# Low parts of singly used weight blocks by an accumulating DMA in place of a DVE subtraction

## The chip, the cores and the metric

One core of a Trainium2 chip runs the whole program in one launch. The metric is the device time of one execution in microseconds (us); lower is better.

## The reference

The reference runs two layers of a hybrid backbone, in float32, over 640 tokens: 512 latent tokens and 128 context tokens, which share all weights. Cut to what matters:

```python
def mixer(h, p, rope, ctx_kv):
    z = h @ p['w_in']
    u_pool, cb, cc, ch, q, k, v, gates = jnp.split(z, [...], axis=-1)
    ...
    g = jax.nn.sigmoid(gates).reshape(B, L, N_BRANCH, D_MODEL)
    merged = (g[:, :, 0] * (pool_out @ p['w_br_pool'])
              + g[:, :, 1] * (conv_out @ p['w_br_conv'])
              + g[:, :, 2] * (attn_out @ p['w_br_attn']))
    return merged @ p['w_o'], k, v

def layer(x, cvec, p, rope, ctx_kv):
    mod = jax.nn.silu(cvec) @ p['w_ada'] + p['b_ada']
    sh1, sc1, g1, sh2, sc2, g2 = [m[:, None, :] for m in jnp.split(mod, 6, axis=-1)]
    h = rmsnorm(x, p['norm1_g']) * (1 + sc1) + sh1
    out, k, v = mixer(h, p, rope, ctx_kv)
    x = x + g1 * out
    h2 = rmsnorm(x, p['norm2_g']) * (1 + sc2) + sh2
    ffn = (jax.nn.silu(h2 @ p['w_gate']) * (h2 @ p['w_up'])) @ p['w_down']
    return x + g2 * ffn, k, v
```

The width is 1024 and the FFN's hidden width 2816. The outputs are both groups' final activations and the new keys and values.

## The kernel before

**Products.** Activations stand transposed, features on the 128 partitions and the 640 tokens in the free dimension, in two halves of 320. A weight block is 128 output features of one matrix: 128 partitions with 1024 columns (8 chunks of 128), or 768 or 512 of them. TensorE multiplies in a rounded 32-bit type (F32R). To keep float32's accuracy each operand is split into a high part, its rounding, and a low part, the rest, and three products are added: high x high, low x high, high x low. So a block of 8 chunks takes 2 x 8 x 3 = 48 matmuls of 320 columns (`mm`, L682).

**The way of a weight block.** `plan` lists all blocks in the order of use. For a block that is used once (`Unit`), SP loads the raw values into one of four RAW buffers (tile `wr`); when two of six WQ buffers (tile `wq`, one for the high and one for the low part) are free, ACT casts the block to the high part (L351) and DVE subtracts that from the raw block into the low part (L352), both in `half_split`. Then the RAW buffer goes back and PE may start. After its last matmul the two WQ buffers go back. The first block of a layer and the first of its FFN (`big`) take one large buffer (`g`) instead. There are 196 such blocks. The first three of the program carry a `gate`, an event that holds their load back until the start has issued its own loads.

```python
    def half_split(hi, lo, src, n):
        yield act(n, lambda: nc.scalar.copy(hi, src), slack=WEIGHT)
        yield dve(n, lambda: nc.vector.tensor_sub(lo, src, hi), slack=WEIGHT)
```

Most gate and up blocks of the FFN come as a `Pair`: their quarters and four sums of quarters serve 7 products in place of 8 (L585), each quarter in one WQ buffer. Their splits also use `half_split`.

**The stages of a layer.** First 14 blocks of w_in for keys, values, queries, pooling and convolution, with attention between them. Then the merge: for each of 8 output blocks m three gate blocks (8 chunks), a branch block that holds the pool's and the convolution's 2 chunks each, and an attention block of 4 chunks; behind each of the three branch products DVE multiplies by the gate (L1479) and adds up (L1485), and the sum is split again (L300 on ACT, L301 on DVE). PE takes them, from the third m on, in the order gate, pool, gate, convolution, gate, attention, that is 48 + 12 + 48 + 12 + 48 + 24 = 192 matmuls. Then 8 blocks of w_o, and the FFN in four groups of gate and up blocks, each followed by 8 down blocks (6 chunks, in the last group 4).

**The modulation (ada).** The vectors mod = silu(c) @ w_ada are not made on PE, but in the background, mostly during the merges: `ada_back` loads half rows of w_ada (256 KB, tile `p`, two buffers) and DVE reduces each against the two conditioning vectors with a fused multiply and sum (L752, tile `junk`, one call for each vector).

```python
            yield d
            while quiet[0]:
                yield 500.0
            for v in range(2):
                ...
                yield ttr(out, w, s[v][q], start, 512, BACK)
            yield 700.0
            PP.put(i)
```

**What sets the order.** The kernel's code is a set of generators. When the program is built, `_Order` runs them against assumed costs (in ns) and lays down each engine's instructions in the order of its own clock. An operation names its engine and cost, `slack` moves its rank in the queue (BACK puts the reductions behind all else), and LAG is added before the next step of the same generator. A load of n bytes is booked at n / 350 ns on a queue `dma` plus 2100 of LAG. On the chip each engine keeps that order and waits on semaphores where data are not there. So a change of one assumed cost moves the order on all engines. SP's queue carries all loads in one order (L284); POOL has only a few small operations.

## Time and profile before

| what | value |
|---|---|
| time, median of 3 runs (lowest to highest) | 1877.96 us (1876.62 to 1879.35) |
| the profiled execution's own time | 1883.69 us |
| its span | 1881.7 us |
| PE, DVE, ACT, POOL busy, share of the span | 97%, 76%, 43%, 2% |
| plain DMA queue | 194.86 MB, 31.7% of the 16 engines |
| HBM read | 188.01 MB |

The span is the time from the first to the last instruction; the profiled execution's time is 2 us longer, and 5.7 us longer than the median of the runs. Busy shares are means over stages that differ, and a busy PE is not always at its peak, so the rows below are taken by stretch. All loads are issued by SP, none by POOL.

### The profile page before, as it was taken

What the parts mean: (1) busy time and instruction counts of PE and PEld (TensorE: products, weight loads), DVE (VectorE), ACT (ScalarE), POOL (GpSimd) and SP (SyncE); (2) the same over time, 40 slices, a digit from 0 to 9 for tenths busy, and PEclk for the clock granted to TensorE, in tenths of its full rate; (3) what the DMA queues carried; (4) which work ended last, traced back from release to release, by engine and by line L of the source; (5) the groups of instructions that cost most, each with busy time, mean ns of one, the idle gap of its engine ahead of it and who ended that gap; (6) DMA issues with size and microseconds to landing.
All of it is one profiled execution on the core that took longest, in us unless ns stands there. A gap on an engine that the chain in (4) does not pass through costs nothing.

```text
span 1881.7 us, 31312 instructions
## 1 busy us (share of the span) xinstructions
PE 1827.1 (97%) x12427; PEld 1794.6 (95%) x12427; DVE 1424.9 (76%) x2663; ACT 816.6 (43%) x1437; POOL 40.1 (2%) x79
## 2 busy tenths in 40 slices
PE   7999999998999999999999999999999999999997
PEld 4999999998989999999989999999999899999997
DVE  7798777887799785775778986888748858667575
ACT  5587622222364252442466775222235525335254
POOL 0100000000000000000002000000000000000000
PEclk9999999999999999999999999999999999999998
DMA  8210144555413322222242012554541222222221
GB/s 321 85 36 31 49 159 146 166 159 205 138 45 116 115 85 84 79 82 81 70 154 74 32 40 80 168 168 165 172 134 35 79 85 85 81 78 83 85 68 68
DMA packets 77107, 196.84 MB, mean 105 GB/s; under 512 B 8865, under 2 KB 12961, under 8 KB 76961
## 3 DMA queue, kind: packets, MB, share of 16 engines
q1 hardware_dynamic: 76962, 194.86, 31.7%
q8 instruction: 97, 1.59, 0.3%
q14 instruction: 48, 0.39, 0.1%
HBM read 188.01 MB, written 5.51 MB: 103 GB/s over the span
## 4 chain that ended last, share of the span: by engine, by line
PE 68%; DVE 17%; DMA 8%; issue 4%; ACT 2%; POOL 0%; SPq 0%; DVEq 0%; POOLq 0%; ACTq 0%
PE ps L682 35%; PE ps L585 25%; DMA p<-in_w_ada 7%; DVE junk L752 5%; DVE wq L352 4%; PE ps L1199 2%; PE ps L1237 2%; PE ps L1217 2%; DVE u L1485 1%; DVE t L1479 1%; PE ps L1672 1%; DVE g L555 1%; PE ps L1010 1%; DVE g L298 0%; DVE g L301 0%
## 5 line engine op out<-in xcount | busy, mean ns | idle before, releaser
L682 PE MATMUL ps<-g,wq 128*128 128x320 f32 x7488 | 1150.0, 310 | 16.9 <-DVE wq L352 6.7
L682 PEld LDWEIGHTS ps<-g,wq 128*128 128x128 f32 x7488 | 1106.9, 188 | 24.2 <-DVE wq L352 10.2
L585 PE MATMUL ps<-g,wq 128*128 128x320 f32 x3360 | 500.8, 311 | 7.3 <-DVE wq L352 4.8
L585 PEld LDWEIGHTS ps<-g,wq 128*128 128x128 f32 x3360 | 497.4, 189 | 9.7 <-DVE wq L352 5.6
L351 ACT CAST wq<-wr 128x512 fp32r<-128x512 f32 (+2 forms) x312 | 244.6, 784 | 314.3 <-PE ps L682 241.9
L352 DVE TENSOR_TENSOR wq<-wr,wq 128x512 fp32r<-128x512 f32 (+2 forms) x312 | 278.0, 891 | 46.6 <-ACT wq L351 45.5
L1524 DVE SCALAR_TENSOR_TENSOR g<-ps,mod,g 128x128 f32<-128x128 f32 (+3 forms) x172 | 83.3, 523 | 160.6 <-PE ps L682 160.6
L752 DVE CUSTOM_DVE_ANT_0 junk<-p,k,vec 128x512 f32<-128x512 f32 x160 | 120.0, 750 | 49.2 <-DMA p<-in_w_ada 46.0
L351 ACT CAST wq<-u 128x512 fp32r<-128x512 f32 x160 | 98.8, 621 | 123.9 <-PE ps L585 59.2
L752 DVE CUSTOM_DVE_ANT_0 junk<-p,k,part 128x512 f32<-128x512 f32 x160 | 120.0, 750 | 27.4 <-DMA p<-in_w_ada 23.8
L352 DVE TENSOR_TENSOR wq<-u,wq 128x512 fp32r<-128x512 f32 x160 | 109.3, 688 | 22.5 <-ACT wq L351 21.8
L1474 ACT ACTIVATE t<-ps 128x640 f32<-128x640 f32 x32 | 22.6, 705 | 176.2 <-PE ps L682 176.2
L642 ACT COPY t<-ps 128x320 f32<-128x320 f32 x80 | 34.2, 427 | 75.7 <-PE ps L585 75.7
L1207 ACT ACTIVATE p<-ps,st 128x640 f32<-128x640 f32 x64 | 51.0, 796 | 25.4 <-DVE st L1205 22.6
L298 DVE TENSOR_TENSOR g<-ps,g 128x640 fp32r<-128x640 f32 (+1 forms) x68 | 54.8, 809 | 5.9 <-ACT g L297 5.5
L916 ACT ACTIVATE g<-t,mod,gain 128x320 fp32r<-128x320 f32 (+5 forms) x108 | 55.6, 572 | 5.7 <-DVE t L897 3.3
L1205 DVE TENSOR_REDUCE st<-ps 128x1 f32<-128x640 f32 x64 | 52.2, 815 | 3.9 <-PE ps L1199 3.6
L297 ACT CAST g<-ps 128x640 fp32r<-128x640 f32 (+1 forms) x68 | 46.4, 684 | 19.9 <-PE ps L1217 16.4
L300 ACT ACTIVATE g<-u 128x640 fp32r<-128x640 f32 x16 | 11.8, 739 | 94.9 <-DVE u L1485 94.9
L301 DVE SCALAR_TENSOR_TENSOR g<-t,g 128x640 fp32r<-128x640 f32 x44 | 36.2, 823 | 17.7 <-ACT g L300 17.7
L1199 PE MATMUL ps<-k,g 128*128 128x320 f32 x256 | 48.9, 313 | 0.3 <-ACT p L1207 0.2
L647 DVE TENSOR_TENSOR t<-t,ps 128x320 f32<-128x320 f32 x80 | 38.7, 484 | 10.3 <-PE ps L585 7.8
(157 smaller groups left out, 1442.1 us busy)
## 6 DMA issues: line engine op xcount, KB each, us to landing
p<-in_w_ada SPq DMA_DIRECT2D x160, 256.0 KB, 2.9
wr<-in_w_in SPq DMA_DIRECT2D x76, 512.0 KB, 3.6
wr<-in_w_gate SPq DMA_DIRECT2D x44, 512.0 KB, 3.3
wr<-in_w_up SPq DMA_DIRECT2D x44, 512.0 KB, 3.3
wr<-in_w_down SPq DMA_DIRECT2D x48, 384.0 KB, 3.1
g<-in_w_ada SPq DMA_DIRECT2D x16, 512.0 KB, 8.3
wr<-in_w_br SPq DMA_DIRECT2D x32, 256.0 KB, 2.7
wr<-in_w_o SPq DMA_DIRECT2D x16, 512.0 KB, 3.4
```

Of the source, the lines that this page charges most:

```text
L297: yield act(n, lambda: nc.scalar.copy(hi, src))
L298: yield dve(n, lambda: nc.vector.tensor_sub(lo, src, hi))
L351: yield act(n, lambda: nc.scalar.copy(hi, src), slack=WEIGHT)
L352: yield dve(n, lambda: nc.vector.tensor_sub(lo, src, hi), slack=WEIGHT)
L585: nc.tensor.matmul(out, lhsT=wt[q][:, k * P : k * P + P], rhs=x.get(t, lo, k), start=start and k == 0 and i == 0, stop=stop and k == 3 and ...
L682: nc.tensor.matmul(toks(ps, c0, n), lhsT=wt[:, c], rhs=xt[:, c0 : c0 + n], start=start and i == 0, stop=stop and i == 2,)
L752: return dve(n + 60, lambda: nc.vector.tensor_tensor_reduce(out=waste[:, :n], in0=w, in1=s, scale=0.5, scalar=start, op0=ALU.mult, op1=ALU ...
L916: nc.scalar.activation(out, sl, AF.Identity, bias=bias, scale=scale)
L1199: nc.tensor.matmul(toks(ps, c0, n), lhsT=qs, rhs=kt[:, c0 : c0 + n], start=j == 0, stop=j == 1)
L1205: yield dve(TOK, lambda: nc.vector.tensor_reduce(st[:, 0:1], toks(ps), axis=AX.X, op=ALU.max, negate=True))
L1207: yield act(TOK + 140, lambda: nc.scalar.activation(pp, toks(ps), AF.Exp, bias=st[:, 0:1], accum_out=st[:, 1:2]))
L1524: yield dve(n, lambda: nc.vector.scalar_tensor_tensor(xs, toks(ps, s0, n), mods[l][:, v, seg * KC + m : seg * KC + m + 1], xs, op0=ALU.mul ...
```

## The change

For the 193 single blocks without a `gate` the low part is made another way (`far_split`). ACT casts the raw block to the high part as before, and then a second time with the scale -1 into the low part's buffer, so that it holds the negated rounding. Then POOL issues a DMA that reads the same weight block from HBM again and adds it to what the buffer holds: raw - high. The RAW buffer goes back as soon as ACT has read it twice. DVE has no part in it. The planner books the issue at 1100 on POOL and 4000 until the low part has landed. The three gated blocks and the pairs keep `half_split`.

```diff
+    def far_split(hi, lo, src, whence, n, raw_done=None):
+
+        yield act(n, lambda: nc.scalar.copy(hi, src), slack=WEIGHT)
+        yield act(n, lambda: nc.scalar.activation(lo, src, AF.Copy, scale=-1.0), slack=WEIGHT)
+        if raw_done:
+            raw_done.fire()
+        yield _Op({"pool": 1100.0}, lambda e: nc.gpsimd.dma_start(
+            out=lo, in_=whence.bitcast(F32R), accum_op=ALU.add), slack=WEIGHT)
+        yield 4000.0
+
     def raw_block(u, src, n, done):
         s = yield RAW.get()
         u.raw.append((s, mk("wr", s, (D,))))
@@ -381,8 +391,13 @@
                 self.placed.fire()
                 self.hi, self.lo = (mk("wq", s, (D,), F32R) for s in self.slots)
             s, raw = self.raw[0]
-            yield from half_split(self.hi[:, :n], self.lo[:, :n], raw[:, :n], n)
-            RAW.put(s)
+            if self.gate:
+                yield from half_split(self.hi[:, :n], self.lo[:, :n], raw[:, :n], n)
+                RAW.put(s)
+            else:
+                read = event()
+                after([read], lambda: RAW.put(s))
+                yield from far_split(self.hi[:, :n], self.lo[:, :n], raw[:, :n], self.src, n, read)
             self.ready.fire()
```

The 15 new lines shift the line numbers behind them: L752 becomes L767, L1479 becomes L1494, L1485 becomes L1500. The order of all engines is planned anew.

DVE's rows in layer 0's merge, around the third gate of one m, before (`p` is the ada load's buffer, `ISA` the reduction and its readout, `wr` and `wq` the raw block and its parts, `u` and `t` the gate's sum and product, `g` the merged sum's parts):

```order
L352 TENSOR_TENSOR wq_4022<-wr_3811,wq_4021 128x512
L752 ISA junk,mod_74<-p_4005,k_2485,part 128x512
L752 ISA mod_74 128x1
L752 ISA junk,mod_74<-p_4005,k_2571,part 128x512
L752 ISA mod_74 128x1
L1479 SCALAR_TENSOR_TENSOR t_4020<-t_4020,ps_4016 128x640
L752 ISA junk,part<-p_4040,k_2436,vec 128x512
L752 ISA part 128x1
L1485 TENSOR_TENSOR u_3845<-u_3845,t_4020 128x640
L352 TENSOR_TENSOR wq_4060<-wr_3885,wq_4059 128x1024
L301 SCALAR_TENSOR_TENSOR g_2440<-u_3845,g_2438 128x640
```

and with the change, at the same place:

```order
L767 ISA junk,part<-p_4108,k_2405,vec 128x512
L767 ISA part 128x1
L1494 SCALAR_TENSOR_TENSOR t_4104<-t_4104,ps_4099 128x640
L767 ISA junk,part<-p_4108,k_2496,vec 128x512
L767 ISA part 128x1
L1500 TENSOR_TENSOR u_3923<-u_3923,t_4104 128x640
L767 ISA junk,mod_74<-p_4126,k_2446,part 128x512
L767 ISA mod_74 128x1
L767 ISA junk,mod_74<-p_4126,k_2538,part 128x512
L767 ISA mod_74 128x1
L301 SCALAR_TENSOR_TENSOR g_2409<-u_3923,g_2407 128x640
```

The two subtractions are gone, and between the gate's product and the merged sum's low part stand three reductions in place of one.

ACT's rows of the same stage, before:

```order
L1474 ACTIVATE u_3845<-ps_3772 128x640
L351 CAST wq_3846<-wr_3678 128x1024
L1474 ACTIVATE t_3929<-ps_3860 128x640
L351 CAST wq_3930<-wr_3697 128x512
L351 CAST wq_3953<-wr_3764 128x1024
L1474 ACTIVATE t_4020<-ps_3947 128x640
```

and with the change:

```order
L1489 ACTIVATE u_3923<-ps_3846 128x640
L356 CAST wq_3924<-wr_3741 128x1024
L357 ACTIVATE wq_3925<-wr_3741 128x1024
L1489 ACTIVATE t_4011<-ps_3940 128x640
L356 CAST wq_4012<-wr_3762 128x512
L357 ACTIVATE wq_4013<-wr_3762 128x512
L356 CAST wq_4033<-wr_3834 128x1024
L357 ACTIVATE wq_4034<-wr_3834 128x1024
L1489 ACTIVATE t_4104<-ps_4026 128x640
```

Each cast is now followed by its negated twin. POOL's rows, which had nothing of this, for the same blocks:

```order
L360 DMA wq_3925<-in_w_in 128x1024
L360 DMA wq_4013<-in_w_br 128x512
L360 DMA wq_4034<-in_w_in 128x1024
L360 DMA wq_4106<-in_w_br 128x512
L360 DMA wq_4146<-in_w_in 128x1024
```

They write the tiles that ACT has just filled, one for each block, in the order of the blocks.

## Rows read from the trace of the kernel before

**Rows 1.** page, its head and part 1 (busy us, share of span, instructions)

```profile
span 1881.7 us, 31312 instructions
...
PE 1827.1 (97%) x12427; PEld 1794.6 (95%) x12427; DVE 1424.9 (76%) x2663; ACT 816.6 (43%) x1437; POOL 40.1 (2%) x79
```

**Rows 2.** busy us (x instructions) of PE, PEld, DVE, ACT, POOL; clock, DMA share, GB/s

```profile
258.00:465.00 207.00, 197.69 (x1330) 194.93 (x1328) 165.98 (x355) 47.31 (x62) 0.00 (x0) 0.99 0.51 165
...
1160.00:1350.00 190.00, 188.43 (x1280) 187.38 (x1279) 154.02 (x330) 46.69 (x62) 0.00 (x0) 1.00 0.51 164
1480.00:1845.00 365.00, 364.53 (x2484) 364.01 (x2483) 246.97 (x412) 146.20 (x253) 0.00 (x0) 1.00 0.25 79
...
1000.00:1100.00 100.00, 99.73 (x723) 97.49 (x723) 93.67 (x163) 73.59 (x143) 9.46 (x31) 1.00 0.15 48
```

**Rows 3.** chain in the first FFN: start us, length us, what

```profile
649.42 73.92 PE ps L585 x504
```

**Rows 4.** waits in 258 to 465 us: engine waited for, total us, times, longest

```profile
DVE junk L752 <- DMA p<-in_w_ada: 38.0, 24, 3.1
PE ps L682 <- DVE wq L352: 5.0, 6, 1.1
```

**Rows 5.** chain in 1160 to 1350 us, its shares by line

```profile
by line: DMA p<-in_w_ada 30.4%; DVE junk L752 24.2%; DVE wq L352 13.6%; issue 13.6%; DVE u L1485 5.2%; DVE t L1479 4.4%; DMA k<-in_cvec 2.9%; DVE u L1479 1.7%; DVE part L752 1.1%; DVE mod L752 1.0%; PE ps L682 0.9%; DVE g L301 0.7%; SPq L28
```

**Rows 6.** DVE groups in 1160 to 1350 us: busy us, mean ns | idle before

```profile
L752 DVE CUSTOM_DVE_ANT_0 junk<-p,k,vec 128x512 f32<-128x512 f32 x64 | 48.0, 750 | 17.8 <-DMA p<-in_w_ada 16.5
L752 DVE CUSTOM_DVE_ANT_0 junk<-p,k,part 128x512 f32<-128x512 f32 x63 | 47.3, 750 | 13.6 <-DMA p<-in_w_ada 12.1
L352 DVE TENSOR_TENSOR wq<-wr,wq 128x1024 fp32r<-128x1024 f32 (+1 forms) x33 | 33.3, 1009 | 0.0
L1485 DVE TENSOR_TENSOR u<-u,t 128x640 f32<-128x640 f32 x13 | 10.6, 819 | 0.0
L1479 DVE SCALAR_TENSOR_TENSOR t<-t,ps 128x640 f32<-128x640 f32 x13 | 10.6, 816 | 0.0
```

**Rows 7.** DMA queue and issues in 1200 to 1300 us: count, KB, median us to landing

```profile
q1 hardware_dynamic: 7762, 16.73, 51.0%
p<-in_w_ada SPq DMA_DIRECT2D x37, 256.0 KB, 2.8
wr<-in_w_in SPq DMA_DIRECT2D x10, 512.0 KB, 4.1
```

**Rows 8.** the ada loads alone, 1200 to 1300 us

```profile
DMA to landing us min/median/max: 2.5/2.8/4.2
```

**Rows 9.** DMA queue and issues in the first FFN, 650 to 930 us

```profile
q1 hardware_dynamic: 6929, 21.80, 24.4%
wr<-in_w_up SPq DMA_DIRECT2D x14, 512.0 KB, 3.3
wr<-in_w_down SPq DMA_DIRECT2D x16, 384.0 KB, 3.1
wr<-in_w_down SPq DMA_DIRECT2D x6, 256.0 KB, 2.6
```

**Rows 10.** the two split instructions by shape, whole run, and an ACT scaling

```profile
L351 ACT CAST wq<-wr 128x1024 fp32r<-128x1024 f32 x96 | 100.5, 1047 | 110.3 <-PE ps L682 80.4 <-issue 26.8 <-DMA wr<-in_w_in 2.8
L351 ACT CAST wq<-wr 128x768 fp32r<-128x768 f32 x48 | 40.0, 834 | 124.8 <-PE ps L682 120.9 <-ACT wq L351 3.9
L351 ACT CAST wq<-wr 128x512 fp32r<-128x512 f32 x168 | 104.0, 619 | 79.2 <-PE ps L682 40.6 <-PE ps L585 35.0 <-issue 1.9
L300 ACT ACTIVATE g<-t 128x640 fp32r<-128x640 f32 x44 | 32.3, 739 | 19.8 <-DVE t L1919 19.8
...
L352 DVE TENSOR_TENSOR wq<-wr,wq 128x1024 fp32r<-128x1024 f32 x96 | 117.0, 1219 | 12.8 <-ACT wq L351 12.0
L352 DVE TENSOR_TENSOR wq<-wr,wq 128x512 fp32r<-128x512 f32 x168 | 115.3, 686 | 22.7 <-ACT wq L351 22.4
L352 DVE TENSOR_TENSOR wq<-wr,wq 128x768 fp32r<-128x768 f32 x48 | 45.6, 950 | 11.1 <-ACT wq L351 11.1
```

## The prediction

> **What bounds the kernel now.** I read part 1 of the page first, then busy time by stretch, then the chain and waits inside the stretches, and last the durations. PE is busy for 97% of the span [rows 1], so time is lost or won only where PE can stand still. In the second FFN it is busy for 364.5 of 365 us [rows 2], and one stretch of the chain holds 504 matmuls of 320 columns in 73.92 us [rows 3]: 146.7 ns each. At that pace a block of 8 chunks (48 matmuls) takes 7.04 us, a whole m of the merge (192) 28.16 us. A faster DVE gives nothing there.
>
> The merge is the stretch to look at. In layer 0 PE is busy 197.7 of 207 us, in layer 1 188.4 of 190 [rows 2]; together 9.3 + 1.6 = 10.9 us are lost. DVE stands still there mostly for one cause: the L752 reductions wait for the ada loads, 38.0 us of 207 [rows 4]. In layer 1 the chain goes through the ada load (30.4%) and L752 (24.2%), with the subtraction at L352 next (13.6%) [rows 5]. So the merge is already close to being paced by a loop: an ada load lands in one of two buffers, DVE reduces it twice, SP loads that buffer again. DVE's order is fixed, so a gate's arithmetic written behind a reduction waits for that reduction's load, and with it the PSUM tiles that PE needs.
>
> **What is removed and added.** 193 of 196 single blocks change: 97 of 1024 columns, 48 of 768, 48 of 512. DVE loses 97 x 1.219 + 48 x 0.950 + 48 x 0.686 = 197 us; ACT gains about 97 x 1.05 + 48 x 0.83 + 48 x 0.62 = 172 us if a scaling copy costs what the cast does [rows 10], and some 15% more by the scaling at L300 (739 ns for 640 columns, so 1.18 us for 1024). ACT is busy 47 of 207 us in the merge; where it is fullest, near 1000 to 1100 us, it has 73.6 of 100 and DVE 93.7 [rows 2]. With at most 14 blocks (100 / 7.04) in that stretch ACT would come to 90 and DVE to 77. Both stay below PE, so I cost this exchange at nothing; if ACT's queue filled, attention's exponentials would be late next.
>
> POOL gets 193 issues. No row shows one. The change's own planner books 1.1 us for each, 0.2 us of lag and 4.0 us until it has landed, 5.3 us. It books a plain 512 KB load at 1.5 + 2.1 = 3.6 us, and rows show 3.3 to 4.1 [rows 7, 9], so I trust its scale and take 5.3. The bounds are 3.3 (a plain load) and 1.1 + 8.2 (twice the slower plain load, if both sides are read in turn). POOL's power operations stand in the same queue, but they are few and POOL is busy 2% [rows 1]. The Trainium skill, DMA: Bandwidth & Descriptors, section "Anatomy of one DMA — SWDGE (gpsimd) path", fits 2.0 us plus bytes over 436 GB/s, an estimate of 3.2 us for 512 KB; by that, rival 2 below would be out and the sum unchanged, but its fit is not of an accumulating transfer, and no run here shows one.
>
> **Is the low part in time?** Three pairs of WQ buffers circulate. From the release of a pair to the low part's landing: 1.05 + 1.18 + 0.2 of hand-overs + 5.3 = 7.7 us; before it was about 1.05 + 1.22 + 0.2 = 2.5. The cover is what PE still has to do on the two other pairs: 14.1 us among full blocks, and least for the second gate of an m, whose buffers come free with the last attention block of the m before: one gate block and the 12 pool matmuls, 60 x 0.1467 = 8.8 us. 7.7 fits into 8.8. Behind the pairs of an FFN group the first down block has 4 products, 7.04 us, for 0.83 + 0.95 + 0.2 + about 4.9 = 6.9: just. So PE does not wait, by 1.1 us in the merge and 0.1 us there. That is zero in the sum.
>
> **What the merge then costs.** Two things happen to the ada loop. First, the planner fills DVE's free time with it: counted in DVE's rows between the 4th and the 24th gate of layer 0, there were 135 reductions and are now 160, so 24 for an m in place of 20, 12 loads in place of 10. Two buffers must give 12 loads in 28.16 us, so one buffer's cycle may be 28.16 / 6 = 4.69 us. Second, the same 2.10 MB of weights that an m loads (three blocks of 512 KB, two of 256) is read a second time, 74.5 GB/s more. The plain queue moves 16.73 MB in 100 us there and holds 51.0% of the 16 engines for it [rows 7], which is 328 GB/s if full, so this is 23 points of share if a byte counts once, and 45 if the destination's read counts too.
>
> The cycle now: 37 loads in 100 us [rows 7] are 2.70 us each, 5.41 us for a buffer; of it 2.8 is the load [rows 8], 1.6 the two reductions with readout (2 x 0.75 [rows 6]), leaving 1.0 of waiting for DVE. L352 is over half of what else DVE does there (33.3 against 10.6 + 10.6 [rows 6]), so I halve the wait: 0.5. With an unchanged load the cycle would be 2.8 + 0.5 + 1.6 = 4.9, or 29.4 us for an m: already 1.2 over PE's 28.16. The load itself will not stay: a 512 KB load takes 3.3 us beside 24.4% share and 4.1 beside 51.0%, a 256 KB load 2.6 and 2.8 [rows 7, 9]. That is 0.2 to 0.8 us for 27 points, and 23 to 45 points come on top. I take 0.4, between the two, nearer the row of the same size; the ends are 0 and 1.4 (every load as late as the latest of rows 8, 4.2 us).
>
> The cycle is then 3.2 + 0.5 + 1.6 = 5.3 us, an m takes 31.8 us, 3.64 over PE. 292 reductions lie in the merges of the two layers (172 and 120), 12.2 m's worth: 12.2 x 3.64 = 44 us. The 10.9 us that PE lost there before are inside the new pace, so 44 - 11 = **33 us slower**. Against the profiled execution's 1883.7 us this is 1917; the median of the runs is 5.7 us lower, 1878.0, so I forecast **1911 us**. Ends of the load: 2.8 gives 12.2 x 1.24 - 11 = +4 (1882), 4.2 gives 12.2 x 9.64 - 11 = +107 (1985).
>
> **Rivals.** *2, late low parts, slower.* With a landing of 8.2 us behind a 1.1 us issue the merge's second gate has its low part after 11.7 us, 2.9 past its cover, once for each m: 16 x 2.9 = 46. The first down block of a group, landing after 6.2 us (twice 3.1 [rows 9]), misses its 7.04 by 2.2 us in 6 places, and those of 4 chunks (5.2 us, twice 2.6) by 0.8 in 16: 26. About 72 us, 1950. It decides from a total of 6.4 us on (8.8 - 2.4). Against it: the planner's 5.3. For it: both the source and the destination must be read. There is also a way for DVE to delay the issue itself, by the longest operation it has in a merge, 0.82 us [rows 6]: 7.7 would become 8.5, still inside 8.8. The Trainium skill, SBUF — State Buffer, section "SBUF: two separate sides", says that POOL cannot write descriptors while DVE holds the port they share, and gives a copy as the operation that does; the rows of the merge show no copy on DVE, and no run here shows such a stall.
>
> *3, the second read is hidden, no change.* The engines are half idle [rows 7]; if the loads keep 2.8 us and DVE's waits shrink to 0.3, the cycle is 4.7, PE's own pace, and the old loss merely stays: 1878.
>
> *4, faster.* If the waits vanish altogether with the subtractions (the chain's 13.6% [rows 5]) and the loads land in under 3.1 us, the loop runs ahead of PE, 2.9 + 0.1 + 1.6 = 4.6 against 4.69, and PE recovers the 10.9 us: 1867. PE also waits for L352 itself there, 5.0 us [rows 4], which is part of that. It decides at load plus wait = 3.1 us.
>
> That the change does not do what it says would show as POOL issues cut into many small transfers; that is rival 2 with a higher price.
>
> **Numbers.** Forecast 0.50, rival 2 0.15, rival 3 0.15, rival 4 0.20. What a measurement here tells from no change is about 0.2%, 3.8 us. Slower 0.65, same 0.15, faster 0.20. The range from 1866 to 1970 takes in rivals 3, 4 and most of the forecast and of rival 2; beyond it lies every load at its latest.
>
> **What would show it.** Right: FFN stretches at the same 146.7 ns a matmul; the merges some 30 and 20 us longer; ada loads at 3.1 to 3.4 us; DVE's idle time there still before L752; no PE wait named after the accumulating DMA of more than a few us. The queue of POOL carries about 83 MB. Wrong: merges at 28.2 us an m (rivals 3, 4), or PE waiting for lows at L682 (rival 2), which also shows as landings beyond 6 us.

## The result, and the profile after

The changed kernel takes 2036.68 us (median of 4 runs, 2033.23 to 2044.62), the kernel before 1878.07 beside it; the ratio is 1.0849, 95% interval 1.0824 to 1.0874. It is slower, as forecast, but by 159 us, where 33 were forecast and the range ended at 1970. The two profiled executions lie closer together, 149.6 us apart by their spans: before's was 5.7 us over its median, this one, 2033.23 us, is 3.4 under. The stages below are measured against these 150. The head of its page, part 1 and part 3 (queue: packets, MB, share of 16 engines):

```profile
span 2031.3 us, 31786 instructions
...
PE 1867.3 (92%) x12427; PEld 1827.5 (90%) x12427; DVE 1263.4 (62%) x2493; ACT 951.0 (47%) x1607; POOL 206.8 (10%) x272
...
q1 hardware_dynamic: 76962, 194.86, 29.6%
q0 software_dynamic: 27792, 82.33, 24.0%
...
HBM read 270.32 MB, written 5.51 MB: 136 GB/s over the span
```

The engines' work moved mostly as planned: DVE is relieved of 161 us [rows 1] and ACT has 134 more. The prediction worked out 197 and 172; by the counts of instructions the new order also moves 23 operations from ACT to DVE. POOL's queue carries the 82 MB. But PE's share falls from 97% to 92%, and q0 needs nearly as much of the DMA engines as q1 does, for less than half the bytes.

To see where the time went, I cut each trace at the same places in PE's work: the products whose matmuls PE issues at L682 (L697 after) come in a fixed number for each stage of a layer, 672 for the names (the 14 blocks of w_in with attention between), 1536 for the merge, 384 for w_o and 1248 for the FFN. Stage lengths in us:

| kernel | names 0 | merge 0 | w_o 0 | FFN 0 | names 1 | merge 1 | w_o 1 | FFN 1 | span |
|---|---|---|---|---|---|---|---|---|---|
| before | 218 | 236 | 65 | 444 | 169 | 236 | 57 | 457 | 1881.7 |
| changed | 219 | 282 | 80 | 456 | 185 | 279 | 67 | 463 | 2031.3 |

The merges lose 46 and 43 us, **89 in all; the other stages lose 60**: w_o 15 + 10, the FFN 12 + 6, the second names 16, the first 1. So most of the loss is where the forecast put all of it, and a good part is where it put none. These are lengths between two matmuls; a count of lost time by stage, which corrects them a little, stands below. Busy time by stretch (us of PE, PEld, DVE, ACT, POOL; clock, DMA share, GB/s), for the merge, w_o and the FFN of layer 0, and the merge of layer 1:

```profile
219.00:501.00 282.00, 243.43 (x1539) 240.03 (x1538) 159.95 (x383) 87.99 (x117) 34.19 (x40) 0.92 0.74 195
501.00:582.00 81.00, 63.34 (x399) 62.15 (x399) 42.49 (x106) 27.46 (x41) 8.61 (x10) 0.87 0.73 200
582.00:1038.00 456.00, 438.49 (x2945) 434.99 (x2944) 284.08 (x504) 213.78 (x370) 33.25 (x38) 0.99 0.44 110
...
1222.00:1501.00 279.00, 242.47 (x1549) 238.98 (x1548) 135.59 (x313) 89.36 (x118) 34.83 (x40) 0.93 0.73 184
```

In the merge the DMA share is 0.74 in place of 0.51 [rows 2], and the granted clock, 0.99 and 1.00 before, is 0.92 and 0.93: beside the stalls there are stretches in which a matmul of 320 columns starts 0.267 us after the one before, in place of 0.147, as the lower of the clock's two levels (1.2 and 2.4 GHz) is granted: from 378 to 384 us, around the end of the stall shown below, in which PE stands from 374.1 to 378.9, the granted clock is 0.50. Counted over the whole trace by the gaps that follow matmuls of 320 columns, from start to start (0.22 to 0.34 us slow, over that a stall; what lies over 0.147 is counted), stalls cost 163 us (41 before) and slow matmuls 51 (21 before): 122 + 30 = 152 is about the whole loss. Three quarters of the slow matmuls start within 10 us behind a stall of over 1 us.

The same count by stage, of all gaps, differs from the table, because attention's matmuls can cross its cuts: 57 of them, some 6 us of work, stand in the second names and no longer in the second merge, and 30 in the first names and no longer in the first merge. By lost time (stalls and slow matmuls) **the merges lose 49 us each, 98 in all, and the other stages 52**: w_o 16 + 9, the FFN 12 + 7, the second names 9, the first gain 1. Where "by lost time" stands below, it is this count.

Waits in the merge of layer 0 (engine, waited for: us in total, times, longest):

```profile
DVE junk L767 <- DMA p<-in_w_ada: 102.0, 54, 5.0
...
ACT g L300 <- DVE u L1500: 76.3, 7, 12.7
...
PE ps L697 <- DMA wq<-in_w_in: 38.1, 12, 6.1
```

DVE's wait for ada loads has grown to 102.0 us, from 36.2 in the same stage before (38.0 in the stretch of [rows 4]). PE waits for the accumulating DMA, which stands where L352 stood with 5.0 us in [rows 4]. And ACT waits for the merged sum, up to 12.7 us at a time. Before, in 218 to 454 us, these waits of DVE and ACT were:

```profile
ACT g L300 <- DVE u L1485: 42.9, 7, 7.8
DVE junk L752 <- DMA p<-in_w_ada: 36.2, 24, 3.1
```

The DMA queues and issues in 290 to 490 us, six full m of that merge (issues: count, KB, median us to landing), and the landing of the ada loads alone:

```profile
q1 hardware_dynamic: 13316, 28.71, 42.8%
q0 software_dynamic: 3917, 11.34, 31.9%
...
p<-in_w_ada SPq DMA_DIRECT2D x65, 256.0 KB, 3.3
wq<-in_w_in POOLq DMA_DIRECT2D x16, 512.0 KB, 7.2
wr<-in_w_in SPq DMA_DIRECT2D x14, 512.0 KB, 5.1
```

```profile
DMA to landing us min/median/max: 2.5/3.3/8.0
```

The ada load's median is 3.3 us, close to the 3.2 that the prediction took, against 2.8 in [rows 8]. Its longest is 8.0 against 4.2, and the mean, over the 55 of the 65 whose landing the trace gives, is 3.88; 10 of them take over 5 us (before, in 290 to 450 us, 1 of 45, with a mean of 3.10). The accumulating transfer of 512 KB takes 7.2 us.

One stall of PE followed back, the timeline of the changed kernel from 365 to 379 us (start, length, engine, line, instruction, idle time before it and its cause):

```profile
366.57 0.75 DVE L767 CUSTOM_DVE_ANT_0 junk<-p,k,vec 128x512 f32<-128x512 f32 x1 [3.08 <-DMA p<-in_w_ada]
...
368.65 0.82 DVE L1500 TENSOR_TENSOR u<-u,t 128x640 f32<-128x640 f32 x1
...
369.50 0.74 ACT L300 ACTIVATE g<-u 128x640 fp32r<-128x640 f32 x1 [12.27 <-DVE u L1500]
...
370.73 1.04 ACT L356 CAST wq<-wr 128x1024 fp32r<-128x1024 f32 x1
...
371.67 1.06 ACT L357 ACTIVATE wq<-wr 128x1024 fp32r<-128x1024 f32 x1
...
373.13 0.88 POOL L360 DMA_DIRECT2D wq<-in_w_in  x1 [14.60 <-ACT wq L357]
...
378.95 2.50 PE L697 MATMUL ps<-g,wq 128*128 128x320 f32 x8 [4.82 <-DMA wq<-in_w_in]
```

A late ada load holds a reduction, behind it in DVE's order stands the merged sum (L1500), for that ACT waits at L300, and behind L300 in ACT's order stand the next gate's cast and negation. From the cast's start to PE's start are 8.2 us. Before, at the same place of the order, the way of the low part was not much shorter, since there the subtraction stood in DVE's order behind reductions; one such place in layer 1, from the timeline of the kernel before:

```profile
1231.20 0.74 ACT L300 ACTIVATE g<-u 128x640 fp32r<-128x640 f32 x1 [5.73 <-DVE u L1485]
...
1232.43 1.04 ACT L351 CAST wq<-wr 128x1024 fp32r<-128x1024 f32 x1
...
1236.96 1.22 DVE L352 TENSOR_TENSOR wq<-wr,wq 128x1024 fp32r<-128x1024 f32 x1
```

Here 5.7 us pass from the cast's start to the low part; with casts and subtractions paired in their order, the five full m of layer 0 show 7.4 to 8.0 us at this place, and the changed kernel 8.0 to 9.7. So what has changed most in the merge is not the way from the cast to the low part, but how late ACT gets to the cast.

### The profile page after: what moved, and what is told of

The parts are those of the page before. It is cut to its first block, busy times and chain, and to the rows that moved or that the text cites. A ratio compares the mean times of both kernels' runs of the same rounds, so it can differ in the third digit from the quotient of the medians.

```text
span 2031.3 us, 31786 instructions
## 1 busy us (share of the span) xinstructions
PE 1867.3 (92%) x12427; PEld 1827.5 (90%) x12427; DVE 1263.4 (62%) x2493; ACT 951.0 (47%) x1607; POOL 206.8 (10%) x272
## 3 DMA queue, kind: packets, MB, share of 16 engines
q1 hardware_dynamic: 76962, 194.86, 29.6%
## 4 chain that ended last, share of the span: by engine, by line
PE 60%; DMA 18%; DVE 9%; issue 8%; ACT 3%; POOL 0%; SPq 0%; DVEq 0%; POOLq 0%; ACTq 0%
PE ps L697 33%; PE ps L600 22%; DMA p<-in_w_ada 9%; DMA wq<-in_w_in 5%; DVE junk L767 3%; DMA wq<-in_w_down 2%; PE ps L1252 1%; DMA wq<-in_w_o 1%; PE ps L1214 1%; PE ps L1232 1%; PE ps L1687 1%; DVE g L298 1%; DMA wq<-in_w_gate 1%; DVE st L1220 1%; ACT p L1222 0%
## 5 line engine op out<-in xcount | busy, mean ns | idle before, releaser
L697 PE MATMUL ps<-g,wq 128*128 128x320 f32 x7488 | 1194.4, 317 | 129.2 <-DMA wq<-in_w_in 77.9
L697 PEld LDWEIGHTS ps<-g,wq 128*128 128x128 f32 x7488 | 1141.6, 194 | 145.8 <-DMA wq<-in_w_in 84.7
L600 PE MATMUL ps<-g,wq 128*128 128x320 f32 x3360 | 497.2, 309 | 5.8 <-DVE wq L352 4.8
L600 PEld LDWEIGHTS ps<-g,wq 128*128 128x128 f32 x3360 | 494.8, 188 | 7.3 <-DVE wq L352 5.3
L356 ACT CAST wq<-wr 128x1024 fp32r<-128x1024 f32 (+2 forms) x190 | 167.8, 883 | 201.5 <-issue 135.4
L767 DVE CUSTOM_DVE_ANT_0 junk<-p,k,part 128x512 f32<-128x512 f32 x160 | 120.1, 751 | 110.1 <-DMA p<-in_w_ada 107.0
L767 DVE CUSTOM_DVE_ANT_0 junk<-p,k,vec 128x512 f32<-128x512 f32 x160 | 120.1, 750 | 97.0 <-DMA p<-in_w_ada 93.9
L357 ACT ACTIVATE wq<-wr 128x1024 fp32r<-128x1024 f32 (+2 forms) x190 | 169.9, 894 | 8.0 <-PE ps L600 8.0
L360 POOL DMA_DIRECT2D wq<-in_w_down x64 | 55.9, 874 | 799.1 <-DVE t L662 475.4
L352 DVE TENSOR_TENSOR wq<-u,wq 128x512 fp32r<-128x512 f32 x160 | 109.2, 687 | 22.9 <-ACT wq L351 22.2
L360 POOL DMA_DIRECT2D wq<-in_w_in x72 | 63.5, 881 | 446.6 <-ACT wq L357 364.8
L351 ACT CAST wq<-wr 128x512 fp32r<-128x512 f32 (+1 forms) x122 | 76.6, 628 | 58.8 <-PE ps L600 33.8
L352 DVE TENSOR_TENSOR wq<-wr,wq 128x512 fp32r<-128x512 f32 (+1 forms) x122 | 84.7, 695 | 11.9 <-ACT wq L351 11.7
L300 ACT ACTIVATE g<-u 128x640 fp32r<-128x640 f32 x16 | 11.8, 737 | 154.5 <-DVE u L1500 154.5
L662 DVE TENSOR_TENSOR t<-t,ps 128x320 f32<-128x320 f32 x80 | 38.8, 484 | 38.7 <-PE ps L600 36.2
L854 ACT ACTIVATE t<-g 128x320 f32<-128x320 f32 (+1 forms) x63 | 29.1, 491 | 59.9 <-DVE g L1539 47.5
```

The lines of the kernel that those rows point to most:

```text
L357: yield act(n, lambda: nc.scalar.activation(lo, src, AF.Copy, scale=-1.0), slack=WEIGHT)
L360: yield _Op({"pool": 1100.0}, lambda e: nc.gpsimd.dma_start(out=lo, in_=whence.bitcast(F32R), accum_op=ALU.add), slack=WEIGHT)
L600: nc.tensor.matmul(out, lhsT=wt[q][:, k * P : k * P + P], rhs=x.get(t, lo, k), start=start and k == 0 and i == 0, stop=stop and k == 3 and ...
L662: yield dve(HA, lambda: nc.vector.tensor_add(dst, dst, self.ps[b][1]))
L697: nc.tensor.matmul(toks(ps, c0, n), lhsT=wt[:, c], rhs=xt[:, c0 : c0 + n], start=start and i == 0, stop=stop and i == 2,)
L767: return dve(n + 60, lambda: nc.vector.tensor_tensor_reduce(out=waste[:, :n], in0=w, in1=s, scale=0.5, scalar=start, op0=ALU.mult, op1=ALU ...
```

## The experiments

Two questions had to be told apart: does the merge lose by the pace of the ada loop (theory D in the expectations; its loads slowed by the second read is B), or by low parts that come late behind ACT's queue (A; A' says so whatever the ada loop does), or because three pairs of WQ buffers are too few (C)? And what loses outside the merge? All are edits of the changed kernel, but for the last two. Stage lengths of all runs stand in a table behind them.

**1. A plain copy in place of the accumulation.**

```diff
         yield _Op({"pool": 1100.0}, lambda e: nc.gpsimd.dma_start(
-            out=lo, in_=whence.bitcast(F32R), accum_op=ALU.add), slack=WEIGHT)
+            out=lo, in_=whence.bitcast(F32R)), slack=WEIGHT)
```

> The changed kernel with its POOL transfers as plain copies (no addition, so the low part holds the whole weight); order and bytes read from HBM are the same. Theory A (a low part is ready some 8.2 us after its cast, and casts come late because ACT's queue stands behind the merge's split at L300, which waits for DVE, which waits for ada loads): the transfer lands in about 5 us in place of 7.4, each of the 36 stalls is some 2.4 us shorter, the total near 1970 us. Theory B (the second read fills the DMA engines and slows every load): the POOL queue's share falls from 24% to about 13%, loads return to 4.1 us, total near 1920. Theory C (three pairs of WQ buffers are too few for the longer way): as A, near 1970.

Measured: 1936.70 us, ratio 1.0337 (1.0315 to 1.0358). The queue and the issues over the whole run:

```profile
q0 software_dynamic: 27792, 82.33, 13.2%
...
wq<-in_w_in POOLq DMA_DIRECT2D x72, 512.0 KB, 5.2
...
wq<-in_w_down POOLq DMA_DIRECT2D x48, 384.0 KB, 4.1
```

The same bytes from the same queue take 13.2% of a 1935.9 us span, against 24.0% of 2031.3: 3.10 us of the 16 engines for a MB in place of 5.92. A plain byte of q1 takes 29.6% x 2031.3 / 194.86 = 3.09, so an accumulated byte costs 1.92 plain ones. The merges lose 16 and 14 us in place of 46 and 43, and both FFNs are back at 445 and 457. So it is the accumulation, more than POOL's part in it, that is dear: without it 62 of the 159 us are left. The total lies between the 1970 of A and C and the 1920 of B and decides for none of them.

**2. No ada loads.** Only the first two loads of each layer are made, and the reductions read those again.

```diff
...
+                if i not in kept:
+                    w = kept[i] = mk("p", i, (TOK,))[:, :512]
+                    load = dma(w, a["w_ada"][l, m, :, q * 512 : q * 512 + 512], follow=True, done=ld[1])
+                else:
+                    w = kept[i]
+                    load = _Op({"dma": 750.0}, lambda e: None, follow=True, done=ld[1])
...
-                yield dma(w, a["w_ada"][l, m, :, q * 512 : q * 512 + 512], follow=True, done=ld[1])
+                yield load
```

> The changed kernel without the ada loads of the background except the first two (the reductions read those two again and again, so the modulation is wrong); the order of PE, DVE and ACT is the same. A: DVE no longer waits, L300 is early, the stalls behind it go; merges from 280 to about 245 us each, total near 1950. B: also near 1950, by landings of the POOL transfers of about 5.5 us. C: the stalls remain at half or more, total over 1990.

Measured: 1925.62 us, ratio 1.0267 (1.0249 to 1.0284). The merge of layer 0 by stretch, and the issues of the whole run:

```profile
219.00:453.00 234.00, 228.01 (x1537) 225.15 (x1537) 167.14 (x399) 89.94 (x117) 34.90 (x40) 1.00 0.68 149
```

```profile
wq<-in_w_in POOLq DMA_DIRECT2D x72, 512.0 KB, 7.3
```

The low parts land as late as ever, 7.3 us after the issue, and yet both merges are back (234 and 237; by lost time 2 and 7 us are left), the clock too (1.00 and 0.99). So the landing time by itself costs the merge little; the rest needs the ada loop. The total is under the 1950 of A and B, and far under the 1990 that C asked for. The stages outside the merges keep their loss.

**3. The loads flow, but DVE does not wait for them.** The reduction reads the conditioning vector in place of `w`.

```diff
-                yield ttr(out, w, s[v][q], start, 512, BACK)
+                yield ttr(out, s[v][q], s[v][q], start, 512, BACK)
```

> The changed kernel with all ada loads in place, but the reductions read the conditioning vector in place of the loaded row (so the modulation is wrong) and wait for no load. A: DVE is on time, L300 too, merges about 245 us each, total near 1955. B: the engines carry the same bytes or more per time, POOL transfers still land in 7 us or more, total over 2000. C: the stalls remain at half or more, total over 1990.

Measured: 1958.51 us, ratio 1.0435 (1.0396 to 1.0473). The merges of both layers:

```profile
219.00:472.00 253.00, 234.84 (x1537) 229.76 (x1536) 167.38 (x400) 90.03 (x117) 34.89 (x40) 0.98 0.85 222
...
1178.00:1425.00 247.00, 232.66 (x1550) 228.37 (x1549) 135.75 (x313) 90.57 (x119) 34.86 (x40) 0.99 0.83 209
```

With every byte still moved (the DMA share is even higher, 0.85), two thirds of the merges' loss are gone: 17 + 11 us are left of 46 + 43 (by lost time 20 + 17 of 98). So most of it comes in by DVE's waiting. In what is left PE waits for low parts, in layer 0:

```profile
PE ps L697 <- DMA wq<-in_w_in: 15.6, 12, 2.7
```

Run 2, without the traffic of the ada loads, has 4.8 us there; that the traffic makes the difference is likely, not shown, since DVE's waits differ too. The total is near the 1955 of A, where B asked for over 2000 and C for over 1990.

**4. The merged sum's split moved back in ACT's order**, behind the next gate's cast and negation, against the chain of the timeline above.

```diff
                 yield self.mg.made
+                if m < KC - 1:
+                    yield 8500.0
                 yield from split(
```

> The changed kernel with the split of a merged sum (L300) moved in ACT's queue from ahead of the next gate's cast and negation to just behind them; nothing is removed. A: the stall of about 5.3 us that each m has goes or falls below 2 us, total near 1960. B: engines as full as before, total within 15 us of 2037. C: likewise within 15 us of 2037.

Measured: 2015.62 us, ratio 1.0758 (1.0731 to 1.0785): a miss for A. The merges are 275 and 267. The link is cut, but the same block is then late for another reason: its raw load stands in SP's queue behind an ada load that waits for its buffer, lands at 358.4 us, and the cast starts at 358.5, after 6.56 us of idle time that the trace puts down to that load. And PE, which in the changed kernel's merges waits for low parts alone, now waits mostly for PSUM tiles that DVE's gate products (L1494) hold, in layer 0:

```profile
PE ps L697 <- DVE t L1494: 20.0, 5, 5.7
PE ps L697 <- DVE u L1494: 7.8, 3, 5.6
```

So the queues that pass the ada loop are held to its pace; freeing one link shows the next.

**5. Fewer reductions for an m.** The pause in the ada loop, which sets how many reductions the planner puts beside one m, made longer in two steps; DVE's order, counted from one merged sum to the next, holds 24 reductions for an m in the changed kernel, 20 to 21 with a pause of 1500, 14 to 15 with 3000.

```diff
-            yield 700.0
+            yield 1500.0
             PP.put(i)
```

> The changed kernel with one planner number altered: a pause of 1500 ns in place of 700 between the ada jobs, so that the DVE order holds some 20.5 reductions for an m in place of 24; all work is done. Theory D (the merge runs at the pace of the ada loop: a cycle of 6.15 us for a buffer was measured, 12 loads for an m, 36.9 us): an m falls to about 31.5 us, the two merges from 282 and 279 to about 250 each, total near 1975. Theory A' (a merge is held by low parts that land 7.5 us after their issue, whatever ada does): merges over 270, total within 15 us of 2037.

Measured: 1992.09 us, ratio 1.0614 (1.0571 to 1.0658), merges 262 and 260: a miss for both forecasts, between the two, nearer D. One buffer's cycle was 6.67 us there, 5 cycles are 33.4, and an eighth of 262 is 32.8. The stronger step is the same line with `yield 3000.0`:

> The changed kernel with the pause in the ada loop at 3000 in place of 700: 14 to 15 reductions for one m of the merge in place of 24, so 7.3 loads; at the cycle of 6.1 us that the changed kernel shows for one of its two buffers, they take 22 us, less than PE's 28.16 for an m. The accumulating DMAs and their landing stay as they are. If the merge ran at the ada loop's pace, the merges fall from 282 and 279 to 235 to 255 us (234 to 237 with no ada loads at all, 253 and 247 with loads that nobody waits for), and the total to 1930 to 1965. If late low parts hold the merge whatever the ada loop does, the merges stay above 265 and the total above 1990. The loads that are moved out of the merge run beside the FFN, whose low parts may come later for it: up to 10 us.

Measured: 1952.98 us, ratio 1.0412 (1.0394 to 1.0429). The merges of both layers, and the landing of the ada loads in 290 to 440 us:

```profile
217.00:463.00 246.00, 232.06 (x1541) 228.14 (x1539) 117.66 (x264) 90.06 (x117) 34.25 (x40) 0.99 0.80 196
...
1173.00:1420.00 247.00, 234.12 (x1548) 229.51 (x1547) 117.70 (x265) 90.67 (x118) 34.08 (x40) 0.99 0.81 196
```

```profile
DMA to landing us min/median/max: 2.7/4.9/9.4
```

This is inside what D forecast, and far from the other reading. The accumulating DMAs are all there, the DMA share is 0.80, the ada loads land even later (median 4.9 us, mean 5.4), and yet the merges give back 36 and 32 of their 89 us (by lost time 68 of 98), because an m no longer asks for more loads than its two buffers can give: 7.3 loads of 5.4 + 1.6 us in two buffers are 26 us. The clock is back at 0.99 with it. 10 and 11 us stay (by lost time 13 and 17), and PE's waits there are for low parts, in layer 0:

```profile
PE ps L697 <- DMA wq<-in_w_in: 13.4, 10, 3.6
```

**6. The bookings nearer to what was measured**: 6500 for the landing, n + 210 for the reduction, a pause of 1700.

```diff
-        yield 4000.0
+        yield 6500.0
...
-        return dve(n + 60, lambda: nc.vector.tensor_tensor_reduce(
+        return dve(n + 210, lambda: nc.vector.tensor_tensor_reduce(
...
-            yield 700.0
+            yield 1700.0
```

> The changed kernel with three planner numbers set to what was measured: 6500 ns to the landing of an accumulating transfer in place of 4000, 782 ns for a reduction in place of 632, and 1700 ns between ada jobs; same work, another order on all engines. D: about 20.8 reductions for an m, merges near 250 us as with the slower ada alone. If what is left outside the merges (61 us) comes from an order made for too early low parts, FFN, w_o and first blocks also win, total near 1930; if it comes from the landing time itself, which no order shortens, total near 1970.

Measured: 2006.71 us, ratio 1.0701 (1.0664 to 1.0737), a miss. DVE's order holds 22 reductions for an m again, in place of 20.8, likely because the later low parts stretch the planner's own m; that was not looked at by itself. The merges stay at 276 and 272.

**7. The change taken out of the merge, and left in the merge alone.** First the merge's gate and branch blocks (80 of 193) go back to `half_split`; then only they have `far_split`.

```diff
+            self.near = near or bool(gate)
...
-            if self.gate:
+            if self.near:
...
-            plan.append(Unit(a["w_in"][l, B_G + b * KC + m]))
+            plan.append(Unit(a["w_in"][l, B_G + b * KC + m], near=True))
```

> The changed kernel with the gate and branch blocks of the merge (80 of the 193) back on the DVE subtraction; w_o, FFN and the first blocks of a layer keep the accumulating transfer. D and A' both: merges back to about 236 us, total near 1945, that is 60 to 70 us over the kernel before, all of it outside the merges: w_o +25, FFN +19, first blocks +17. If the merges' delay had pushed the other stages, those would shrink too and the total would be under 1915.

Measured: 1926.48 us, ratio 1.0271 (1.0255 to 1.0286), 19 below the forecast of that run, since the merges came out at 228 each, shorter than before. Half of this is attention's work that now stands in the names (by lost time the two merges gain 7 us). Their m have 18 to 22 reductions, as many as before, and most last 28.2 us, PE's own pace.

> The complement of the run that took the change away from the merge: here only the gate and branch blocks of the merge (80 of 193) get their low part by the accumulating DMA, all other single blocks have the DVE subtraction again. If the parts add (merge's loss and the loss outside it have causes of their own), the merges are near 280 us each as in the changed kernel (236 before), names, w_o and FFN stand within 10 us of before, and the total is 1970 to 1990. If the losses feed on each other, the merges come out clearly shorter than 275 and the total under 1950. If w_o still loses (its first blocks are prepared during the merge), that loss belongs to the merge.

Measured: 1986.66 us, ratio 1.0600 (1.0581 to 1.0619). Merge, w_o and FFN of layer 0 in this second run:

```profile
217.00:502.00 285.00, 245.74 (x1554) 241.60 (x1553) 162.85 (x385) 89.43 (x119) 33.55 (x38) 0.93 0.72 193
502.00:567.00 65.00, 60.25 (x398) 59.58 (x397) 48.00 (x104) 20.20 (x34) 0.88 (x1) 0.95 0.49 175
567.00:1010.00 443.00, 437.23 (x2949) 434.31 (x2949) 318.18 (x555) 189.59 (x337) 2.65 (x2) 0.99 0.25 85
```

The two losses have causes of their own. With the change in the merge alone everything outside it stands as before; with the change outside alone w_o, the FFNs and the second names lose 57 us, nearly the changed kernel's 60 (by lost time all stages outside lose 49 and 52). The totals of the two runs, 50 and 112 us over the kernel before, add up to 162, where the changed kernel loses 159.

**8. ACT's second pass by itself.** ACT casts and negates, DVE adds the raw block; no second read, and the RAW buffer goes back after the addition.

```diff
-        yield _Op({"pool": 1100.0}, lambda e: nc.gpsimd.dma_start(
-            out=lo, in_=whence.bitcast(F32R), accum_op=ALU.add), slack=WEIGHT)
-        yield 4000.0
+        yield dve(n, lambda: nc.vector.tensor_add(lo, src, lo), slack=WEIGHT)
...
```

> Half of the change alone: ACT casts and writes the negated rounding, but DVE adds the raw block to it, and there is no second read. If the accumulating transfer is the whole cost, the time is the kernel before's within 10 us (1878); if ACT's second pass of 1.05 us in front of gate work costs too, up to 1 us for each of 193 blocks at the places that wait, total over 1895.

Measured: 1876.86 us, ratio 1.0008 (0.9998 to 1.0017). ACT's 193 negations cost nothing that can be told from zero.

**9. The kernel before with a slower ada loop.** If the loop's pace is what the merge pays for, the kernel before pays it too. Once the pause alone, 1500; once the reduction booked as measured and a pause of 1000 (16 and 18 reductions for an m, in place of 20 to 22).

```diff
-        return dve(n + 60, lambda: nc.vector.tensor_tensor_reduce(
+        return dve(n + 210, lambda: nc.vector.tensor_tensor_reduce(
...
-            yield 700.0
+            yield 1000.0
```

> The kernel before, with one number changed: the pause in the ada loop 1500 in place of 700, so that fewer reductions are planned for one m of the merge. If what PE loses in the merge before (10.9 us in the profiled execution) is the ada loop's pace, most of it comes back: 1866 to 1872 us, with the merges near 230. If those loads only move into stretches where PE then waits, or if the loss has another cause, the time stays within 0.2% of before, 1874 to 1880.

> The kernel before, with the reduction booked at about its measured time (n + 210 in place of n + 60) and the pause at 1000 in place of 700. Same two readings as for the run with the longer pause alone: 1866 to 1872 if the ada loop's pace is what PE loses in the merge, 1874 to 1880 if not; a wrong booking of DVE elsewhere may move the order for the worse.

Measured: 1862.95 us, ratio 0.9933 (0.9921 to 0.9945), and 1860.82 us, ratio 0.9925 (0.9912 to 0.9937): both faster than the kernel before, by 12 and 14 us, and better than the best that was expected, 1866. Merge and w_o of layer 0 in the second:

```profile
209.00:442.00 233.00, 233.00 (x1603) 232.97 (x1602) 176.75 (x360) 67.53 (x96) 0.00 (x0) 1.00 0.44 150
442.00:499.00 57.00, 57.00 (x393) 56.99 (x392) 42.28 (x90) 19.62 (x32) 0.85 (x1) 1.00 0.48 165
```

PE is never idle in them; every m but the first takes 28.2 us. The order is new on all engines, so this is not the number of reductions alone: in the first run of 7 most m keep PE's pace with 18 to 22 of them.

| kernel | names 0 | merge 0 | w_o 0 | FFN 0 | names 1 | merge 1 | w_o 1 | FFN 1 | span |
|---|---|---|---|---|---|---|---|---|---|
| 1, plain copy | 218 | 252 | 72 | 445 | 182 | 250 | 60 | 457 | 1935.9 |
| 2, no ada loads | 219 | 234 | 67 | 457 | 185 | 237 | 67 | 465 | 1930.4 |
| 3, unwaited | 219 | 253 | 71 | 451 | 185 | 247 | 67 | 465 | 1956.9 |
| 4, split later | 217 | 275 | 86 | 451 | 185 | 267 | 68 | 462 | 2010.2 |
| 5, pause 1500 | 219 | 262 | 74 | 457 | 185 | 260 | 67 | 465 | 1987.9 |
| 5, pause 3000 | 217 | 246 | 66 | 459 | 185 | 247 | 71 | 465 | 1955.8 |
| 6, bookings | 221 | 276 | 79 | 451 | 183 | 272 | 70 | 459 | 2012.2 |
| 7, not in merge | 218 | 228 | 76 | 458 | 184 | 228 | 66 | 465 | 1923.7 |
| 7, merge alone | 217 | 285 | 65 | 443 | 169 | 289 | 57 | 457 | 1981.4 |
| 8, no second read | 212 | 233 | 65 | 443 | 166 | 240 | 57 | 458 | 1873.2 |
| 9, before, pause 1500 | 216 | 229 | 57 | 442 | 169 | 233 | 57 | 457 | 1860.4 |
| 9, before, as measured | 209 | 233 | 57 | 443 | 168 | 233 | 57 | 458 | 1858.9 |

## Why the prediction was right in kind and wrong in size

**What bounds the kernel** was right for the changed kernel: its merge runs at the pace of the ada loop (runs 2, 3 and 5). The last two runs bear out that the kernel before already paid for it, in the order that it had: the longer pause alone gives back 7 and 3 us in its merges and 8 in its first w_o, against a profiled execution that was 5.7 us over its median. The link was another than the prediction's. It let PE wait for PSUM tiles that a late gate product holds; in the changed kernel no wait of PE in the merges is for these, but the merged sum holds ACT, and ACT the next low part. The PSUM link shows only when that one is cut (run 4).

**The exchange of DVE for ACT** was rightly costed at nothing (run 8); the negation of 1024 columns takes 1.06 us, like the cast, and not the 1.18 taken.

**The engines' share** lay between 23 and 45 points, depending on how often a byte counts. It counts 1.92 times in engine time (run 1), nearly the upper end. The text kept both ends and then took a load of 3.2 us, "nearer the row of the same size", that is, with the lower end in mind.

**"What the merge then costs"** is the first step that failed, in the size of one term. The formula holds. Of one buffer's cycle, forecast as 3.2 + 0.5 + 1.6 = 5.3 us, the trace shows 6.15 in 290 to 490 us (200 us for 65 loads in two buffers): 3.88 + 0.37 + 1.69 for the 55 loads whose landing is known, 0.03 until SP issues the next load, and 0.2 that is left. Six of them are 36.9 us for an m; the ten m of the two merges with 11 or 12 loads last 36.5 us on average, against 31.8 forecast. With 36.5 the prediction's own sum, 12.2 m times 8.34 us less 11, gives +91, and the merges lost 89 by the table, 98 by lost time. The load was 0.7 too short, and mostly by a choice of statistic: the median did go where it was put, 3.3, but a loop that waits for each load pays the mean, and 10 of 55 take 5 to 8 us. With plain second reads (run 1) the m's of 11 or 12 loads last 32.2 us: what was priced was about what a plain copy does.

**"Is the low part in time?"** is the second step that failed; it was put at zero. The landing was taken as 5.3 us, the planner's booking, "since I trust its scale"; it is 7.4 for 512 KB, over the 6.4 from which rival 2 was to decide, and less than that rival's 1.1 + 8.2. And the cover was counted from the release of the two WQ buffers, as if ACT cast at that moment. ACT casts when its order comes to it: in the merge behind L300, elsewhere behind whatever stands ahead. Nor was the way before 2.5 us in the merge: the trace has 8.9 us from the cast's start to the low part of a 1024-column block (median of 18, 290 to 454 us), because the subtraction stood behind reductions in DVE's order, and 9.8 with the change (median of 17, 290 to 490 us). Outside the merges it did grow: from 2.4 to 12.9 us in the first w_o, from 3.2 to 10.6 in the second names, from 2.3 to 8.3 for the first FFN's blocks of 768 columns. So the way grew most in w_o and the names, where the prediction did not look. The FFN shows the plain form of it, the chain of the changed kernel around the first down block of a group (start, length, what):

```profile
898.81 0.50 DVE t L662
...
899.36 5.34 DMA wq<-in_w_down
...
904.75 5.39 PE ps L697 x35
```

The cast of that block began at 897.4, its negation ended at 899.0, POOL issued at 899.4, and the part landed at 904.7, 0.55 us after PE had run out of products of the pairs. Rival 2 put 26 us on the two FFNs, which lost 18. With w_o and the second names, which it did not name, the stages outside the merges lost 52 by lost time, of which 38 are waits of PE that name an accumulating DMA; in the first w_o another 10.5 (4.2 before) are a wait for L300, behind a late ada load once more. So rival 2 did not take the forecast's place but came on top of it, which the cases, each worked out alone, left no room for. The sum 33 + 72 = 105 would have been nearer than either, though still 45 short of the 150, and in part by luck: 46 of the 72 were put in the merges, where runs 2, 3 and 5 leave 9 to 37 us by lost time to the late parts.

**The clock** had no term. 30 of the 150 us are matmuls at the lower level, 24 of them in the two merges, in stretches with stalls. Where a run takes the stalls away (runs 2 and 5, 0.99 to 1.00 in the merges), the clock is back with them. In the merges it needs no term of its own: six cycles of the loop are 36.9 us already, and an m lasts 36.5.

**What the signs showed.** The FFN's plain stretches hold their pace, DVE's idle time in the merge stands before L767, POOL's queue carries 82 MB, as listed under right; landings beyond 6 us and PE waits at L697 were listed for rival 2. Of the list under right, two signs failed: the merges are 46 and 43 us longer and not some 30 and 20, and PE's waits for accumulating DMAs are 114 us in all, up to 7.1 at once, and not a few.

Of the Trainium skill's fit in DMA: Bandwidth & Descriptors, section "Anatomy of one DMA — SWDGE (gpsimd) path", an estimate of 3.2 us for 512 KB, run 1 shows the plain copy near it only at its fastest: 3.5 us, with a median of 5.2 beside this kernel's other traffic; the accumulating one of 512 KB was never under 5.5. The measured values decide, and they would have put rival 2 into the sum.

What stays open: in the stages outside the merge the order of ACT was not separated from the landing time. Run 1, where a part lands some 2 us sooner, gives back the FFNs and most of w_o's loss, but only 2 of 16 us in the second names, 6 of which are moved work. More WQ buffers, which might hide both, were not tried.

## What to carry to other kernels

When a background loop with few buffers stands in the same order as the critical work, count what it asks for in the time of one step against what its buffers can give at the mean load time, and let the planner ask for less: one number in the kernel before was worth 0.7%. Count the cover of a late operand from where its producer really stands in its engine's order, not from the moment at which its buffer comes free, and read that way off the trace from its first instruction to its last: a sum of durations gave 2.5 us where 8.9 passed. And where two losses have causes of their own, add them; they are not rivals.

## What the runs showed of the hardware

- An accumulating DMA from HBM onto SBUF takes 1.92 times the engine time of a plain one for a byte (5.92 against 3.09 us of the 16 engines for a MB). 512 KB land after 7.4 us in the median (5.5 at the fastest), a plain copy from the same queue after 5.2 (3.5), and 384 KB after 6.3 against 4.1.
- Its issue holds POOL for 0.87 us against 0.53 for a plain copy.
- Landings spread more than their median moves: 256 KB loads of SP's queue take 3.10 us in the mean with a median of 2.9 at a DMA share of 0.50 (before, 290 to 450 us; 1 of 45 over 5 us), and 3.88 with a median of 3.3 at 0.75 (changed, 290 to 490 us; 10 of 55).
- A high DMA share with late landings costs little where the work does not run at the pace of these loads: run 5 with a pause of 3000 has a share of 0.80 and ada loads of 4.9 us in the median, against 0.74 and 3.3 in the changed kernel, and its merges are 36 and 32 us shorter.
